# Where w_out's small sums are issued, and how many splits stand behind each half product of the output projection

## The chip, the core and the metric

The kernel runs on one core of a Trainium2 chip. The metric is device microseconds (us) of one execution. TensorE (PE in the profile) multiplies matrices, VectorE (DVE), ScalarE (ACT) and GpSimd (POOL) work elementwise. SyncE (SP) issues loads and stores; POOL also issues DMAs, those that add to what stands at the target (accumulating DMAs). Each engine takes its instructions in the order in which they are written.

## The reference

One layer of a gated short-convolution mixer between two RMS norms, in float32, for 1024 rows of 1024 channels:

```
u = rms_norm(x, pre_norm)
z, bg, cg, v = split(u @ w_in, 4)            # 1024 -> 4 x 2048
y = bg * causal_dwconv(cg * v, conv_w) * silu(z)
out = x + rms_norm(y @ w_out, post_norm)     # 2048 -> 1024
```

## The kernel before

Every float32 operand of a matmul is split into a high part (cast by ACT) and a low part (what the cast left over, by DVE); a product takes three matmuls, low by high, high by low, high by high. Both projections are made with fewer products than the plain way needs (a Strassen-like scheme): sums of blocks of the operands are multiplied instead of the blocks.

**Input projection.** The 64 column groups of `w_in` (16 channel blocks `c`, four kinds each) are taken three at a time: 20 *triples* `t` after four plain groups at the start. A triple is 20 steps `s`, each one product of six 128x512 matmuls into one of five PSUM chains pV, pW, pX, pY, pZ; ACT or DVE reads a chain before the next product is added to it. The weights of triple `t+1` are prepared during triple `t`: POOL makes 16 groups of sums (`sums`, L166 to L197, one source line each, L181 for group 0 to L196 for group 15), and ACT and DVE split the results in pairs named A to J (`split_w`, L219; A, B and C still in triple `t`, D to J in triple `t+1`). POOL also multiplies the gates (L314, L323, L341). `y` of each finished channel block goes to DRAM (`y_half`, stores by SP), and POOL adds up there the sums of `y` blocks that the output projection needs (`more`, L371).

**Output projection.** Its seven pairs of operands are called a, b, c, e, d, f, g. All but f are two half products `(i, h)` of four row tiles with 12 matmuls of 128x512 each, 48 in a half product. f is a further such scheme of seven parts p on quarter blocks, in the order `FP` = 1, 2, 6, 5, 7, 3, 4, 24 matmuls of 128x256 each; their results stand in three banks pf, read by DVE after each part (L1011, L1013). Parts of f need small sums of `w_out` blocks (`tf_d` in DRAM, made by `small_t`, L427) and of `y` blocks (`sf_d`, `small_s`).

`small_t` has four steps. Step 0: SP copies four quarter blocks of `w_out` to `tf_d`, 512 KB each. Step 1: POOL adds another quarter block to two of them. Step 2: POOL adds one of the results to a third block; it waits for step 1 to land. Step 3: POOL adds that to the fourth; it waits for step 2. Before, they stand in triple 18 (`END - 1`), at steps 2, 15, 18 and 20.

An operand of the output projection is a list of *pieces*, two of u (w_out side) and two of y for a half product, one of each for a part of f, 62 in all. `fetch_unit` loads raw pieces by SP, `ru_` for w_out and `ry_` for y; `split_unit` takes the next piece in order and issues its cast on ACT (L905, or L902 with a sign) and its low part on DVE (L906 or L903). `refill` loads ahead, never more than four pieces further than what is split. The first eight splits (a) stand in triple 19. After that, a fixed number of splits stands in the program behind each half product: four, or two behind each part of f. What is read out of PSUM (`combine`) comes behind these splits; behind f's parts 3 and 4 come the norms and the output rows of the first four row tiles (`finish_row`, DVE lines L96 to L104, L1050, L1070). Raw pieces share six buffers, split pieces and `ry_` tiles share 18.

Of the kernel before, what the change touches and what calls it, by code (L numbers as in the profile page):

```python
# [20 lines left out]
def kernel(  # L21
# [144 lines left out]
    def fetch_triple(t):  # L166
        if t < len(TRIPLES):
            for j, g in sorted(zip(COLS[t], TRIPLES[t]), key=lambda a: (2, 0, 1).index(a[0])):
                ws[t, j] = fetch_w(*g)
# [46 lines left out]
    def run_lows():  # L216
        while lows:
            lows.pop(0)()

    def split_w(t, unit):  # L220

        if t >= len(TRIPLES):
            return
        at = {"w0": ws[t, 0], "w1": ws[t, 1], "w2": ws[t, 2], "e": es[t]}
        x = wp.tile([P, 2, 2 * FC], F32R, tag="w", name=f"w{unit}_{t}", bufs=5)
        ps = bank(f"w{unit}_{t}")
        (i, a, m), (j, b, n) = UNITS[unit]
        if a == b and n == m + 1:
            src = flat(at[a][:, m : n + 1])
            nc.scalar.copy(ps, src)  # L230
            nc.scalar.copy(x[:, 0], src)  # L231
        else:
            nc.scalar.copy(ps[:, :FC], at[a][:, m])
            nc.scalar.copy(ps[:, FC:], at[b][:, n])
            nc.scalar.copy(x[:, 0], ps)  # L235
        lows.append(lambda: nc.vector.tensor_sub(x[:, 1], ps, x[:, 0].bitcast(F32)))  # L236
        wf[t, i], wf[t, j] = (x, 0), (x, FC)

    def product(t, i):

        ch, first = CHAIN[i]
        if first:
            banks[t, ch] = bank(f"p{ch}_{t}")
        x, off = wf.pop((t, i))
        for kk in range(2):
            s = slice(off + kk * P, off + (kk + 1) * P)
            pass3(banks[t, ch], x[:, 0, s], x[:, 1, s], U[i], kk, first and kk == 0, kk == 1)
# [27 lines left out]
    def run_due(at_once=False):  # L275
        moved = True
        while moved:
            moved = False
            for item in list(waiting):
                needs, gives, delay, do = item  # L280
                if all(n in have for n in needs):
                    if at_once or now[0] >= max(have[n] + delay.get(n[1], 0) for n in needs):
                        waiting.remove(item)
                        do()
                        have[gives] = now[0]
                        moved = True
# [59 lines left out]
    def read(t, i):  # L346

        ps = banks[t, CHAIN[i][0]]
        for (col, h), sign in READS.get(i, ()):
            c, ty = TRIPLES[t][COLS[t].index(col)]  # L350
            if (col, h) == (0, 1):
                use(c, ty, h, ps, sign, direct=True)
                continue
            if (t, col, h) not in acc:
                a = acc[t, col, h] = target(c, ty, h)
                if sign > 0:
                    nc.scalar.copy(a, ps)  # L357
                else:
                    nc.scalar.mul(a, ps, -1.0)  # L359
                continue  # L360
            a = acc[t, col, h]
            if sign > 0:
                nc.vector.tensor_add(a, ps, a)  # L363
            else:
                nc.vector.tensor_sub(a, a, ps)  # L365
            if LAST[col, h] == i:
                use(c, ty, h, acc.pop((t, col, h)))


    def more(dst, src):  # L370
        nc.gpsimd.dma_start(dst, src, accum_op=ALU.add)  # L371
# [6 lines left out]
    def run_later():  # L378
        if later and later[0][0] <= now[0]:
            later.pop(0)[1]()  # L380
# [23 lines left out]
    def fetch_t(j):  # L404
        for i, k, e in (("e", 0, 0), ("d", 0, 1), ("c", 1, 1), ("g", 1, 0)):
            nc.sync.dma_start(t_d[:, TK[i], j], wov[:, k * CH + j, e * HB : (e + 1) * HB])
# [14 lines left out]
    def w22(i, j):  # L421
        return quarter(wov, i, j, CH, HB)
# [4 lines left out]
    def small_t(step):  # L427
        if step == 0:
            for n, src in enumerate((w22(0, 0), w22(0, 0), w22(1, 1), w22(1, 0))):
                nc.sync.dma_start(tf_d[:, n], src)  # L430
        elif step == 1:
            more(tf_d[:, 0], w22(0, 1))
            more(tf_d[:, 2], w22(0, 1))
        elif step == 2:
            more(tf_d[:, 1], tf_d[:, 2])
        else:
            more(tf_d[:, 3], tf_d[:, 1])
# [173 lines left out]
    def high_u(i):  # L611
        U[i] = u = new_u(f"u_{i}")
        for kk in range(2):
            if i in FORM:
                nc.scalar.copy(u[:, 0, kk], FORM[i][kk])
            else:
                nc.scalar.copy(as_block(u[:, 0])[:, kk], stage(i)[:, kk])

    def low_u(i, eng=nc.vector, kks=(0, 1)):
        u = U[i]  # L620
        for kk in kks:
            if i in FORM:
                nc.vector.tensor_sub(u[:, 1, kk], FORM[i][kk], u[:, 0, kk].bitcast(F32))
            else:
                eng.tensor_sub(as_block(u[:, 1])[:, kk], stage(i)[:, kk], as_block(u[:, 0])[:, kk].bitcast(F32))
        FORM.pop(i, None)
# [208 lines left out]
    def first_chunk(s):  # L835

        if s == 4:
            silu1.append(snap(2, 1))
        elif s == 5:
            for h, t in ((0, sn0[2]), (1, silu1[0])):  # L840
                nc.gpsimd.tensor_mul(cv_of(0, h), cv_of(0, h), t)
        elif s == 6:
            gate_y(0, 0, sn0[3], 1, False)
        elif s == 19:
            gate_y(0, 1, plain_ps[3, 1], 1, True)

    FP = (1, 2, 6, 5, 7, 3, 4)
# [63 lines left out]
        OP[side, i, h, q] = t  # L911

    END = len(TRIPLES) - 1
    SUMS = {1: (0,), 2: (1,), 3: (2,), 4: (3,), 5: (4,), 6: (5,), 7: (6,), 8: (7,), 9: (8,), 10: (9,), 11: (10,), 12: (11,), 17: (12, 13), 18: (14,), 19: (15,)}
    SPLIT = {2: "D", 3: "E", 6: "F", 8: "G", 9: "H", 11: "I", 13: "J"}
    SPLIT_0 = {1: "F", 2: "G", 6: "H", 7: "E", 11: "I", 13: "J"}
# [5 lines left out]
    for t in range(len(TRIPLES)):  # L922
        for s, i in enumerate(ORDER if t else ORDER_0, 1):
            now[0] += 1
            product(t, i)
            read(t, i)
            run_lows()
            while low_us:
                low_us.pop(0)()
            if t == 0:  # L930
                first_chunk(s)
                if s in LOWS:
                    low_u(LOWS[s][0], kks=LOWS[s][1])
            run_due()
            for unit in (SPLIT if t else SPLIT_0).get(s, ""):
                split_w(t, unit)
            if t == 0 and s in HIGHS:
                high_u(HIGHS[s])
            for unit in (NEXT if t else NEXT_0).get(s, ""):
                split_w(t + 1, unit)  # L940
            sums(t + 1, (SUMS if t or s > 15 else SUMS_0).get(s, ()))
            if s == 14:
                fetch_triple(t + 2)
            if s in (7, 14, 20):
                run_later()
            if 2 <= t < 2 + 2 * CH:
                j = (t - 2) // 2
                if t % 2 == 0 and s == 3:
                    fetch_t(j)
                if t % 2 == 0 and s == 15:  # L950
                    add_t(j, 0)
                if t % 2 == 1 and s in (15, 20):
                    add_t(j, 1 + (s == 20))
            if t == END - 1 and s in (2, 15, 18, 20):
                small_t((2, 15, 18, 20).index(s))
            if t == END - 1 and s == 14 or t == END and s in (2, 8, 13, 15, 17):
                fetch_unit()
            if t == END and s in (6, 9, 11, 13, 15, 17, 19, 20):
                split_unit(True)
# [133 lines left out]
    def finish_row(t):  # L1093
        finish_o(t)
        if t + 2 < NT:
            load_res(t + 2)

    SMALL_S = {("c", 0): 0, ("c", 1): 1, ("e", 0): 2, ("e", 1): 3}
    for n, (i, h) in enumerate(OUT[:-2]):
        if (i, h) == ("f", FP[0]):  # L1100
            load_res(0)
            load_res(1)
        if i == "f":
            small_mm(h)
        else:
            for q in range(TH):
                out_mm(i, h, q)
        for z in range(2 if i == "f" else 4):
            split_unit()
            refill()  # L1110
        if (i, h) in SMALL_S:
            small_s(SMALL_S[i, h])
        if i != "f" and h == 1:
            for q in range(TH):
                combine(i, q)
        if i == "f" and h in (3, 4):
            for q in (0, 1) if h == 3 else (2, 3):
                norm_square(q, 1)
                finish_row(q)
# [33 lines left out]
```

## Time and profile before

| | us |
|---|---|
| median of 3 runs (lowest, highest) | 782.32 (779.84, 782.43) |
| the profiled execution | 782.2 |
| its span | 780.4 |
| PE busy in the span | 761.1 |
| triple 18, triple 19, first matmul | 552.3, 579.5 |
| first matmul of a, f, g | 615.5, 724.6, 744.7 |
| last matmul ends | 773.4 |

The profiled execution takes 1.8 us more than its span. Times in the text are us from the start of the span. In rows of the timeline the columns are start, duration, engine, line, operation, output<-inputs, count, and in brackets how long the engine sat idle before and what ended that. Views of waits give total, number, longest. In a table by windows each engine has its busy time and its instructions, then the granted TensorE clock, the share of the 16 DMA engines in use, and GB/s. q1 is SP's DMA queue, q0 POOL's.

### The profile page before, as it was taken

The page shows a single profiled execution, that of the slowest core. Times are in us where ns is not written, and L with a number is a line of the kernel's source. Part 1 is how long each engine was busy: PE and PEld are TensorE (multiplying, and loading weights), DVE is VectorE, ACT ScalarE, POOL GpSimd, SP SyncE. Part 2 cuts the span into 40 slices and gives each one's busy share as a digit, 9 for nine tenths or more (in the row PEclk, how much of TensorE's full clock was granted, in tenths as well). Part 3 has the DMA queues.
Part 4 walks back from the last instruction along what each step waited for, and adds up shares of the span by engine and source line. Part 5 has one row for each costly group of instructions (what it writes and reads, how often), then busy time and mean ns, then how long its engine had stood idle before and what let it go on. Part 6 is the DMA issues. An engine that isn't in the chain of part 4 may idle for free.

```text
span 780.4 us, 10226 instructions
## 1 busy us (share of the span) xinstructions
PE 761.1 (98%) x3458; PEld 632.6 (81%) x3458; DVE 498.4 (64%) x761; ACT 459.1 (59%) x887; POOL 471.3 (60%) x576
## 2 busy tenths in 40 slices
PE   9999999999999999999999999999999799999976
PEld 8888888888888888888888888888887588888965
DVE  6898766565656555664756575656654856456894
ACT  8869746555755665665565566657555554445641
POOL 0678978777876786696797869778853311100030
PEclk9999999999999999999999999999999899999998
DMA  9402346448165455364574763665768699967555
GB/s 326 134 1 68 95 126 145 135 85 231 37 188 122 133 140 132 95 161 122 122 203 81 178 146 95 149 175 112 206 116 213 220 343 393 299 175 257 207 197 203
DMA packets 111684, 128.10 MB, mean 164 GB/s; under 512 B 5080, under 2 KB 78096, under 8 KB 110864
## 3 DMA queue, kind: packets, MB, share of 16 engines
q1 hardware_dynamic: 99136, 104.37, 40.8%
q0 software_dynamic: 12480, 23.07, 18.0%
q8 instruction: 27, 0.44, 0.2%
q14 instruction: 25, 0.20, 0.1%
q10 hardware_dynamic: 16, 0.00, 0.0%
HBM read 108.56 MB, written 52.43 MB: 206 GB/s over the span
## 4 chain that ended last, share of the span: by engine, by line
PE 87%; DMA 4%; POOL 3%; DVE 2%; issue 2%; ACT 1%; SPq 0%; DVEq 0%; POOLq 0%; ACTq 0%
PE pX L135 7%; PE pX L136 7%; PE pX L137 7%; PE pY L136 6%; PE pY L135 6%; PE pY L137 6%; PE po_x L987 4%; PE po_x L988 4%; PE po_x L989 4%; PE pV L136 3%; PE pV L135 3%; PE pV L137 3%; PE pW L136 2%; PE pZ L136 2%; PE pW L137 2%; PE pZ L137 2%
## 5 line engine op out<-in xcount | busy, mean ns | idle before, releaser
L365 DVE TENSOR_TENSOR sn<-sn,pY 128x512 f32<-128x512 f32 x57 | 39.2, 687 | 56.4 <-PE pY L137 28.8
L341 POOL TENSOR_TENSOR g<-g,sn 128x512 f32<-128x512 f32 x29 | 40.6, 1406 | 35.0 <-ACT sn L339 28.1
L365 DVE TENSOR_TENSOR sn<-sn,pX 128x512 f32<-128x512 f32 x57 | 39.3, 689 | 33.6 <-PE pX L137 33.5
L314 POOL TENSOR_TENSOR g<-sn,g 128x512 f32<-128x512 f32 x23 | 30.0, 1305 | 44.1 <-DVE sn L363 44.1
L339 ACT ACTIVATE sn<-sn 128x512 f32<-128x512 f32 x24 | 15.2, 632 | 63.1 <-DVE sn L365 39.1
L359 ACT ACTIVATE sn<-pV 128x512 f32<-128x512 f32 x38 | 20.6, 596 | 48.0 <-PE pV L137 48.0
L1051 POOL TENSOR_TENSOR res<-xr,res 128x512 f32<-128x512 f32 x4 | 6.8, 1706 | 65.9 <-DVE res L1050 65.9
L323 POOL TENSOR_TENSOR g<-g,sn 128x512 f32<-128x512 f32 x20 | 28.3, 1414 | 19.2 <-DVE sn L365 18.9
L357 ACT COPY sn<-pZ 128x512 f32<-128x512 f32 x19 | 11.2, 589 | 46.7 <-PE pZ L137 46.7
L371 POOL DMA_DIRECT2D s_d<-s_d x24 | 20.0, 835 | 21.5 <-DMA s_d<-y_d 13.8
L181 POOL TENSOR_TENSOR raw<-raw 128x256 f32<-128x256 f32 x40 | 32.3, 920 | 0.0
L363 DVE TENSOR_TENSOR g<-pY,g 128x512 f32<-128x512 f32 x15 | 10.4, 692 | 30.7 <-PE pY L137 30.7
L186 POOL TENSOR_TENSOR raw<-e,raw 128x256 f32<-128x256 f32 x40 | 28.8, 741 | 1.6
L182 POOL TENSOR_TENSOR e<-raw,raw 128x512 f32<-128x512 f32 x20 | 26.2, 1311 | 1.6
L135 PE MATMUL pp<-b,wn 128*128 128x512 f32 x62 | 24.6, 397 | 0.0
L136 PE MATMUL pp<-b,wn 128*128 128x512 f32 x62 | 24.4, 393 | 0.0
L137 PE MATMUL pp<-b,wn 128*128 128x512 f32 x62 | 24.2, 390 | 0.0
L304 DVE SCALAR_TENSOR_TENSOR g<-g,cw,cv 128x512 f32<-128x512 f32 x30 | 22.5, 749 | 1.7
L236 DVE TENSOR_TENSOR wE<-wE,wE 128x512 fp32r<-128x512 f32 x20 | 13.7, 687 | 14.0 <-ACT wE L235 14.0
L304 DVE SCALAR_TENSOR_TENSOR cv<-g,cw,cv 128x512 f32<-128x512 f32 x30 | 22.4, 748 | 0.0
L135 PE MATMUL pX<-b,wJ 128*128 128x512 f32 x40 | 16.3, 408 | 6.1 <-DVE sn L365 6.1
L236 DVE TENSOR_TENSOR wC<-wC,wC 128x512 fp32r<-128x512 f32 x20 | 13.8, 688 | 11.9 <-ACT wC L231 11.9
(409 smaller groups left out, 2961.3 us busy)
## 6 DMA issues: line engine op xcount, KB each, us to landing
raw<-in_sc_w_in SPq DMA_DIRECT2D x64, 512.0 KB, 4.5
t_d<-in_sc_w_out SPq DMA_DIRECT2D x32, 256.0 KB, 4.4
s_d<-g SPq DMA_DIRECT2D x29, 256.0 KB, 2.1
s_d<-s_d POOLq DMA_DIRECT2D x24, 256.0 KB, 4.7
y_d<-g SPq DMA_DIRECT2D x23, 256.0 KB, 2.6
t_d<-in_sc_w_out POOLq DMA_DIRECT2D x16, 256.0 KB, 7.4
t_d<-t_d POOLq DMA_DIRECT2D x16, 256.0 KB, 5.0
xr<-in_x SPq DMA_DIRECT2D x8, 512.0 KB, 5.6
```

What stands on the lines that cost most here:

```text
L135: nc.tensor.matmul(ps, lo, u[:, 0, kk], start=first, stop=False, skip_group_check=True)
L136: nc.tensor.matmul(ps, hi, u[:, 1, kk], start=False, stop=False, skip_group_check=True)
L137: nc.tensor.matmul(ps, hi, u[:, 0, kk], start=False, stop=last, skip_group_check=True)
L181: 0: lambda: (add(w2[:, 0], w2[:, 0], w2[:, 1]), add(w2[:, 2], w2[:, 1], w2[:, 2])),
L186: 5: lambda: (sub(w0[:, 2], e[:, 3], w0[:, 2]), sub(w0[:, 0], e[:, 3], w0[:, 0])),
L304: nc.vector.scalar_tensor_tensor(g if j == TAPS - 1 else ps, g, tap(c, j), ps, op0=ALU.mult, op1=ALU.add)
L314: nc.gpsimd.tensor_mul(g, src, g)
L341: when([(c, "cv", h), (c, "silu", h)], (c, "z", h), {"cv": 1, "silu": 1}, lambda: nc.gpsimd.tensor_mul(cv_of(c, h), cv_of(c, h), t))
L365: nc.vector.tensor_sub(a, a, ps)
L987: nc.tensor.matmul(ps, lo, u[:, 0, k % 2], start=first, stop=False, skip_group_check=True)
L988: nc.tensor.matmul(ps, hi, u[:, 1, k % 2], start=False, stop=False, skip_group_check=True)
L989: nc.tensor.matmul(ps, hi, u[:, 0, k % 2], start=False, stop=last, skip_group_check=True)
```

## The change

```diff
@@
     END = len(TRIPLES) - 1
+    SMALL_T = ((END - 2, 3), (END - 1, 2), (END - 1, 6), (END - 1, 10))
...
-            if t == END - 1 and s in (2, 15, 18, 20):
-                small_t((2, 15, 18, 20).index(s))
+            if (t, s) in SMALL_T:
+                small_t(SMALL_T.index((t, s)))
@@
+    SPLITS = {("e", 0): 5, ("e", 1): 5, ("d", 0): 6, ("d", 1): 6, ("f", 3): 0, ("f", 4): 0}
+    SPLITS.update({("f", p): 2 for p in FP[:4]})
+    SPLITS["f", 7] = 0
...
-        for z in range(2 if i == "f" else 4):
+        for z in range(SPLITS.get((i, h), 4)):
             split_unit()
             refill()
```

The four steps of `small_t` move from triple 18's steps 2, 15, 18, 20 to triple 17's step 3 and triple 18's steps 2, 6, 10. On SP the four copies now stand in front of the three `w_in` loads of triple 19 instead of behind them and three stores. Behind e's half products stand five splits each instead of four, behind d's six, behind f's first four parts two each as before, and none behind its last three. So f's part 1 is split behind e, its parts 2, 6, 5 and 7, 3, 4 behind d, and g's eight pieces behind f's parts 1, 2, 6 and 5, in front of the output rows. SP's two loads of x rows now come behind the loads of g's first half.

POOL, from the end of triple 18's sums to triple 19's first gate, before (`raw_`, `e_`: weights and sums of triple 19; `g_0_5063`, `g_1_5038`: gates of channel block 14):

```order
L192 TENSOR_TENSOR raw_0_5168<-e_5257,raw_0_5168 128x256
L371 DMA s_d<-s_d 128x512
L371 DMA tf_d<-in_sc_w_out 128x4x256 x2
L341 TENSOR_TENSOR g_1_5038<-g_1_5038,sn_0_1_5375 128x512
L193 TENSOR_TENSOR e_5257<-e_5257,raw_3_5172 128x256
L194 TENSOR_TENSOR raw_3_5172<-raw_3_5172 128x256
L341 TENSOR_TENSOR g_0_5063<-g_0_5063,sn_0_0_5253 128x512
L195 TENSOR_TENSOR e_5257<-e_5257,raw_1_5170 128x256
L371 DMA tf_d<-tf_d 128x1024
L196 TENSOR_TENSOR raw_1_5170<-raw_1_5170 128x256
L371 DMA s_d<-s_d 128x512
L371 DMA tf_d<-tf_d 128x1024
```

Behind the last of these stands the gate `L323 g_0_5063`. POOL now, from the second group of sums on:

```order
L182 TENSOR_TENSOR e_5261<-raw_0_5172,raw_1_5174 128x512
L371 DMA tf_d<-in_sc_w_out 128x4x256 x2
L183 TENSOR_TENSOR e_5261<-e_5261,raw_1_5174 128x256
L184 TENSOR_TENSOR raw_3_5176<-raw_0_5172,raw_3_5176 128x256
L266 MEMSET g_0_5316 128x2
L185 TENSOR_TENSOR e_5261<-raw_3_5176 128x256
L186 TENSOR_TENSOR raw_1_5174<-e_5261,raw_1_5174 128x256 x2
L371 DMA tf_d<-tf_d 128x1024
L187 TENSOR_TENSOR raw_1_5174<-raw_1_5174 128x256
```

and further on:

```order
L190 TENSOR_TENSOR raw_0_5172<-raw_3_5176,raw_0_5172 128x256
L371 DMA tf_d<-tf_d 128x1024
L191 TENSOR_TENSOR raw_3_5176<-raw_3_5176,e_5261 128x256
L192 TENSOR_TENSOR raw_0_5172<-e_5261,raw_0_5172 128x256
L371 DMA s_d<-s_d 128x512
L341 TENSOR_TENSOR g_1_5038<-g_1_5038,sn_0_1_5378 128x512
```

The four `tf_d` DMAs that stood behind the sums of groups 0 to 11 now stand among them, the last in front of groups 10 and 11.

DVE around f's last parts, before (`pf_`: read of a part of f; `ou_g`, `oy_g`: low parts of g's pieces), first the piece with g's first six splits, and then the one with its last two; between the two pieces stand the output rows of tiles 0 and 1:

```order
L906 TENSOR_TENSOR ou_g_6631<-ru_g_6568,ou_g_6631 128x1024
L906 TENSOR_TENSOR ou_g_6634<-ru_g_6570,ou_g_6634 128x1024
L1011 TENSOR_TENSOR res<-pf_6500,res 128x2x256
L906 TENSOR_TENSOR oy_g_6666<-ry_g_6603,oy_g_6666 128x1024
L906 TENSOR_TENSOR oy_g_6669<-ry_g_6603,oy_g_6669 128x1024
L1013 TENSOR_TENSOR res<-res,pf_6605 128x2x256
L903 SCALAR_TENSOR_TENSOR ou_g_6699<-ru_g_6637,ou_g_6699 128x1024
L903 SCALAR_TENSOR_TENSOR ou_g_6702<-ru_g_6639,ou_g_6702 128x1024
```

```order
L1070 SCALAR_TENSOR_TENSOR res<-res,rs_post_6731,xr 128x512
L1013 TENSOR_TENSOR res<-res,pf_6500 128x2x256
L906 TENSOR_TENSOR oy_g_6768<-ry_g_6672,oy_g_6768 128x1024
L906 TENSOR_TENSOR oy_g_6771<-ry_g_6672,oy_g_6771 128x1024
L96 TENSOR_SCALAR ve_post_6777<-so,so_all 128x1
```

DVE at the same place now (its line numbers are one higher):

```order
L1014 TENSOR_TENSOR res<-res,pf_6564 128x2x256
L906 TENSOR_TENSOR oy_g_6590<-ry_g_6508,oy_g_6590 128x1024
L906 TENSOR_TENSOR oy_g_6593<-ry_g_6508,oy_g_6593 128x1024
L1014 TENSOR_TENSOR res<-res,pf_6528 128x2x256
L903 SCALAR_TENSOR_TENSOR ou_g_6623<-ru_g_6560,ou_g_6623 128x1024
L903 SCALAR_TENSOR_TENSOR ou_g_6626<-ru_g_6562,ou_g_6626 128x1024
L1012 TENSOR_TENSOR res<-pf_6629,res 128x2x256
L906 TENSOR_TENSOR oy_g_6655<-ry_g_6596,oy_g_6655 128x1024
L906 TENSOR_TENSOR oy_g_6658<-ry_g_6596,oy_g_6658 128x1024
L1012 TENSOR_TENSOR res<-pf_6528,res 128x2x256
L1014 TENSOR_TENSOR res<-res,pf_6629 128x2x256
L96 TENSOR_SCALAR ve_post_6714<-so,so_all 128x1
```

All low parts of g's pieces now stand in front of the first output row (L96), two between the reads of f's parts 1, 2, 6, 5 and 7.

## The prediction

> **What bounds the kernel now.** I read the page first, then PE's waits, then busy time by stretches, and then the chain of waits over the two places where PE stood still.
>
> ```profile
> PE 761.1 (98%) x3458; PEld 632.6 (81%) x3458; DVE 498.4 (64%) x761; ACT 459.1 (59%) x887; POOL 471.3 (60%) x576
> ```
> ```profile
> PE pX L135 <- DVE sn L365: 6.1, 1, 6.1
> PE po_x L987 <- DVE oy_g L906: 4.9, 1, 4.9
> ```
> ```profile
> 610.20:616.20 6.00, 5.99 (x14) 4.70 (x15) 4.95 (x5) 4.18 (x6) 2.77 (x3) 0.51 0.70 261
> 752.50:756.20 3.70, 3.69 (x9) 2.95 (x10) 3.56 (x12) 0.33 (x2) 1.04 (x1) 0.54 0.67 238
> ```
>
> PE is the bound: it has no wait of size but two, 6.1 and 4.9 us. Behind each it ran on a granted clock of 0.51 for 6.0 us and 0.54 for 3.7 us, which loses 6.0 x 0.49 = 2.9 and 3.7 x 0.46 = 1.7 us. So 6.1 + 2.9 + 4.9 + 1.7 = 15.6 us is all that this change can win: 8.9 in triple 19 and 6.6 in g, rounded. The number of matmuls doesn't change. The Trainium skill ("TensorE: Matmul & The Clock Gate", section "Part 1: The HAM clock gate (the "warmup" mystery)") has the half clock follow an idle window of about 3.4 us; both rows agree, and no run here shows a shorter wait of PE next to that limit.
>
> The chain through the first wait, and through the second:
>
> ```profile
> 593.92 9.46 DMA ry_a<-y_d
> 603.40 1.06 ACT oy_a L905
> 609.56 0.61 DVE sn L365
> 610.21 0.79 PE pX L135
> ```
> ```profile
> 731.06 7.75 DMA ry_g<-y_d
> ...
> 752.51 0.77 PE po_x L987
> ```
>
> First wait: the load of a's y pieces is issued at 593.92 and lands at 603.4. ACT stands at its cast, DVE behind ACT, and the read of pX that PE needs for the last two products is queued on DVE behind the low part of that piece: 610.21 - 603.38 = 6.8 us from landing to PE. Second wait: g's first twelve matmuls ran, and the low part of the second half's y piece came late, since on DVE the output rows of tiles 0 and 1 stand in front of it.
>
> **Triple 18 and 19.** Why is the load late? POOL, before:
>
> ```profile
> 558.67 0.73 POOL L183 TENSOR_TENSOR e<-e,raw 128x256 f32<-128x256 f32 x1
> 566.22 0.74 POOL L191 TENSOR_TENSOR raw<-raw,e 128x256 f32<-128x256 f32 x1
> 568.39 1.55 POOL L371 DMA_DIRECT2D tf_d<-in_sc_w_out  x1
> 576.54 1.25 POOL L371 DMA_DIRECT2D tf_d<-in_sc_w_out  x1 [6.61 <-issue]
> 583.78 0.88 POOL L371 DMA_DIRECT2D tf_d<-tf_d  x1 [1.20 <-DMA tf_d<-in_sc_w_out]
> 590.84 0.81 POOL L371 DMA_DIRECT2D tf_d<-tf_d  x1 [4.66 <-DMA tf_d<-tf_d]
> 591.38 1.60 POOL L323 TENSOR_TENSOR g<-g,sn 128x512 f32<-128x512 f32 x1
> ```
>
> The gate L323 stands behind the fourth DMA, which waited 4.66 us for the third. SP stores the gate's result and then issues ry_a, 593.92 - 591.38 = 2.5 us after the gate starts. Between the four starts lie 8.15, 7.24 and 7.06 us: the second waits 6.61 us for nothing that the profile names, and its start is 8.15 us behind the first, so I take it that POOL holds it until the first is through; the others wait for a landing. In program order these waits are unavoidable wherever the four stand. What changes is what is queued behind them.
>
> The change puts the first at the place of L183, 558.67, 9.7 us earlier; its data are there, since SP has nothing to wait for in front of the four copies. With the same distances the fourth starts at 581.1 instead of 590.84. But behind it now stand the sums of groups 10 and 11, a DMA, two gate products (L341), the groups 12 to 15 and a DMA. L191 (group 10) starts 0.54 us behind the fourth, the time from the fourth to L323 above: at 581.7, and it ends at 582.4, where it ended at 567.0. Who waits for that?
>
> ```profile
> 577.58 0.62 ACT L231 CAST wC<-raw 128x512 fp32r<-128x512 f32 x1
> 581.04 1.09 ACT L359 ACTIVATE sn<-pV 128x512 f32<-128x512 f32 x2 [2.84 <-PE pV L137]
> ```
> ```profile
> 583.56 0.39 PE L135 MATMUL pV<-u,wC 128*128 128x512 f32 x1
> 584.92 0.39 PE L135 MATMUL pY<-b,wC 128*128 128x512 f32 x1
> ```
> ```profile
> 579.76 0.69 DVE L321 SCALAR_TENSOR_TENSOR g<-pX,g 128x512 f32<-128x512 f32 x1 [0.83 <-PE pX L137]
> ```
>
> ACT's two instructions for wC (about 1.1 us) start at 582.4 and its read of pV (1.1) is queued behind them, so it ends at 584.6. PE needs that read for the product at 583.56: 1.0 us late. On POOL L192 and a DMA follow (1.2 us), then the gate L341 of 1.6 us like L323, to 585.2; the DVE gate L321, which needs it, ends at 585.9 and the read of pY behind it at 586.5, against 584.92 + 1.0 for the product that needs it: another 0.6. Cost 1.6 us. It grows one for one if the fourth DMA is later, and is nothing if it is 1.6 us earlier (range 0 to 4). The weights for A and B are late too but needed later than they come.
>
> From the fourth DMA to the gate L323 are now its 0.54 us, six sums (L191 to L196) of 0.74, two gate products of 1.6 and two DMAs of 0.54, 9.3 us in all: the gate starts at 590.4, only 1.0 us earlier than before, and ry_a is issued at 592.9. So the early issue is hardly the gain. The landing is:
>
> ```profile
> s_d<-g SPq DMA_DIRECT2D x1, 256.0 KB, 5.9
> ```
> ```profile
> q0 software_dynamic: 92, 0.30, 57.1%
> ```
> ```profile
> s_d<-g SPq DMA_DIRECT2D x29, 256.0 KB, 2.1
> ```
>
> The store just in front of ry_a took 5.9 us where the 29 of its kind take 2.1, and in the window 590 to 594 only POOL's queue moved anything (0.30 MB, the only queue listed): the fourth DMA, 512 KB, in flight until 598. It now lands near 588, and beside ry_a only one accumulate of 256 KB is left. I take 6 to 8 us for ry_a, 7.0, between 9.46 less the 3.8 us by which the store is over its median, and the 9.46 itself. It lands at 599.9, PE can go on at 606.7. Unhindered PE would be there after 18 products of 1.36 us (583.56 to 584.92) from triple 19's start at 579.5, at 604.0, plus 1.6: 605.6. A wait of 1.1 us is left (0 with a landing in 5.9 us, 3.6 with one in 9.46, and then the slow stretch comes back). Triple 19 wins 8.9 - 1.6 - 1.1 = 6.2 us.
>
> The Trainium skill ("DMA: Bandwidth & Descriptors", section "Anatomy of one DMA — SWDGE (gpsimd) path") gives a POOL-issued DMA about 2.0 us plus its bytes at 436 GB/s, for 512 KB an estimate of 3.2 us. The trace's 7 to 8 us disagree, and the measurement decides; by the page the fourth would start near 568.3, both rests would be nothing, and the time, with the last stage as below, would be 767.7.
>
> On SP the four moved copies now stand ahead of triple 19's three weight loads. I cost them at nothing: four issues, each well under 1 us, in a triple of 27 us whose weights are wanted in the next one.
>
> **The last stage.** DVE during f, before:
>
> ```profile
> 727.66 0.69 DVE L1011 TENSOR_TENSOR res<-pf,res 128x512 f32<-128x512 f32 x1 [0.58 <-PE pf L1006]
> 728.27 1.22 DVE L906 TENSOR_TENSOR ou_f<-ru_f,ou_f 128x1024 fp32r<-128x1024 f32 x1
> 730.54 0.69 DVE L1013 TENSOR_TENSOR res<-res,pf 128x512 f32<-128x512 f32 x1
> ```
>
> ```profile
> 724.59 0.28 PE L1004 MATMUL pf<-ou_f,oy_f 128*128 128x256 f32 x1
> 744.74 0.40 PE L987 MATMUL po_x<-ou_g,oy_g 128*128 128x512 f32 x1
> ```
>
> One read and two low parts take DVE 730.54 - 727.66 = 2.88 us, just what PE takes for a part of f: (744.74 - 724.59) / 7 = 2.88. Before, 14 low parts stood here, six of f and eight of g, and the last two behind two output rows. Now the six stand behind d, and g's eight follow parts 1, 2, 6 and 5. If DVE starts as before, g's last low part ends at 727.66 + 4 x 2.88 = 739.2, and PE wants it at 752.5 - 4.9 = 747.6: the wait and its slow stretch are gone, 6.6 us.
>
> But DVE has no slack in this row of steps: part 6 needs the read of part 1 (one bank), 7 that of 6, 3 that of 5, 4 that of 7. What delays DVE's first read delays PE. And DVE reaches it only behind the six splits and d's four reads. The last of the six waits for the load of part 4's y:
>
> ```profile
> 710.28 1.22 DVE L906 TENSOR_TENSOR oy_f<-ry_f,oy_f 128x1024 fp32r<-128x1024 f32 x1
> ...
> 713.80 1.23 DVE L906 TENSOR_TENSOR oy_f<-ry_f,oy_f 128x1024 fp32r<-128x1024 f32 x1 [1.16 <-ACT oy_f L905]
> ```
> ```profile
> 715.05 0.38 SPq L870 DMA_DIRECT2D ry_f<-s_d  x1
> ```
> ```profile
> ry_f<-s_d SPq DMA_DIRECT2D x1, 512.0 KB, 8.5
> ```
> ```profile
> 716.63 0.69 DVE L1088 TENSOR_TENSOR res<-po_x,res 128x512 f32<-128x512 f32 x1 [1.61 <-PE po_x L989]
> 719.35 0.69 DVE L1088 TENSOR_TENSOR res<-po_x,res 128x512 f32<-128x512 f32 x1 [0.48 <-PE po_x L989]
> ```
>
> The load is issued when the split of 713.80 ends and frees its buffer. Now it needs the buffer freed two splits earlier, by the one of 710.28: 711.5. With 7 us (ry_g's 7.75 is near) to 8.5 us to land and two splits of 1.1 us the first read of d starts at 720.7 to 722.2 instead of 716.63. Each of d's four rounds takes 2.7 us, of which 0.48 is waiting, so 2.25 without: DVE is through at 729.7 to 731.2, and has read part 1 at 730.4 to 731.9. PE starts part 6 at 724.6 + 5.8 = 730.4, so it waits 0 to 1.5 us. I take 1.0 us (range 0 to 4). ry_g waits for a tile that d's last matmuls free, just ahead of 724.6, and lands by 724.6 + 7.75 = 732.3; its low parts stand behind part 2's read, which comes about then. That costs nothing. The last stage wins 6.6 - 1.0 = 5.6 us.
>
> **Sum.** 782.2 - 6.2 - 5.6 = 770.4 us against the profiled execution, which stands 0.1 us from the median of 782.32. For the waits of 1.0 to 1.5 us I add no slow stretch.
>
> **Rivals.** (1) Only the last stage wins. The waits among the sums and a landing of ry_a as slow as before cost what the early start gives: 782.2 - 5.6 = 776.6. For it speaks that the gate comes just 1.0 us earlier; against it the 5.9 us store, which shows what held the load. (2) Only triple 19 wins: DVE's row of steps in f starts 4 us late (the load of 8.5 us becomes one of 12) and passes that to PE with the slow stretch. 782.2 - 6.2 = 776.0. (3) Slower. POOL's chain among the sums takes as long as the same two shapes take later:
>
> ```profile
> 660.09 1.30 POOL L371 DMA_DIRECT2D sf_d<-s_d  x1 [5.97 <-issue]
> 670.23 1.27 POOL L371 DMA_DIRECT2D sf_d<-s_d  x1 [8.84 <-issue]
> 686.16 0.83 POOL L371 DMA_DIRECT2D sf_d<-sf_d  x1 [13.79 <-DMA sf_d<-sf_d]
> ```
>
> There 10.1 us lie between the first two and 15.9 to the third. With 10.1 and then twice 12 (half way between 7.1 and 15.9, rounded) the fourth starts at 592.8 instead of 581.1: PE waits 1.6 + 11.7 = 13.3 us for wC and what hangs on it, with a slow stretch of 2.9, and the rest of 1.1 stays: 17.3 lost where 8.9 was, and 5.6 won, 785.0. It decides from a fourth DMA 8 to 9 us late, about 590. Against it: those three ran beside the loads of the output projection's pieces. (4) Both repairs fail by halves (a PE wait of 4 us at each place, with the slow stretches of 2.9 and 1.7, and the 1.6 at wC: 14.2 of the 15.6 stay), 780.8: no difference that can be told.
>
> **How the numbers follow.** Forecast 0.54, rival 1 0.17, rival 2 0.11, rival 4 0.10, rival 3 0.08. A measurement of this kernel tells about 0.5% from no change, 3.9 us: faster is below 778.4. Faster 0.82, same 0.10, slower 0.08. The forecast's own range is 766 (all 15.6 won) to 775 (rests of 3 us at one place). The range given goes to 765.5, since the runs shown reach 2.4 us below the profiled one, and to 777.5, which takes in rivals 1 and 2.
>
> **What would show it.** The wait of PE for oy_g is gone and the clock is 1.0 behind g's first half. POOL's second tf_d DMA starts 8 us behind the first with 6 to 7 us of idle time, now between L182 and L183; L191 starts near 581.7. PE has a short wait at pV<-u,wC. ry_a is issued near 592.9 and lands by 600. DVE's first read of pf is 2 to 4 us later relative to the start of f. I am wrong if POOL doesn't stand between the first two, if PE's wait in triple 19 stays above 4 us, or if waits over 3 us appear in f.

## The result, and the profile after

The changed kernel takes 769.33 us (median of 4 runs, 767.91 to 770.13) against 781.33 (4 runs, 779.84 to 782.43) for the kernel before: a ratio of 0.9846, 95% interval 0.982 to 0.9871. The forecast was 770.4 (765.5 to 777.5), with 0.82 for faster. Of all executions reported here one, of the kernel before beside e1 to e3, fell far out of line (2294.45 us): the medians take it in, the ratios leave it out.

The page of the changed kernel, then its waits of PE (total, times, longest):

```profile
span 767.9 us, 10230 instructions
...
PE 757.8 (99%) x3458; PEld 630.2 (82%) x3458; DVE 497.5 (65%) x761; ACT 459.1 (60%) x887; POOL 471.3 (61%) x576
```
```profile
PE pw L489 <- DVE idle L459: 1.1, 1, 1.1
PE pX L135 <- DVE sn L365: 0.2, 1, 0.2
```

Both waits of the kernel before are gone but for 0.2 us; the 1.1 us at L489 belong to the start of the kernel and were there before. The slow stretches behind them are gone too. These are the windows of the same lengths behind the two places (length, PE, PEld, DVE, ACT, POOL with their instructions, then the granted clock, DMA share, GB/s):

```profile
605.10:611.10 6.00, 5.99 (x26) 4.99 (x27) 4.95 (x5) 4.18 (x6) 2.78 (x3) 1.00 1.05 345
741.00:744.70 3.70, 3.70 (x18) 3.04 (x18) 2.72 (x8) 1.46 (x5) 1.74 (x1) 1.00 0.81 278
```

In 6.0 us PE does 26 matmuls where it did 14, and in 3.7 us 18 where it did 9, at a clock of 1.00.

Where the 12.5 us between the two spans (780.4 and 767.9) come from is read off the starts of PE's first matmuls of each stage:

| us | before | after | difference |
|---|---|---|---|
| up to triple 19 | 579.48 | 579.91 | +0.43 |
| triple 19 | 36.01 | 28.05 | -7.96 |
| a to d | 109.10 | 108.80 | -0.30 |
| f | 20.15 | 20.42 | +0.27 |
| g, first to last matmul's start | 28.31 | 21.56 | -6.75 |
| from there to the end | 7.35 | 9.16 | +1.81 |

The last row is what no term of the forecast held. POOL's `tf_d` DMAs in triple 18 and the two rows that the forecast named behind them, changed kernel (the rows between are left out):

```profile
558.97 1.26 POOL L371 DMA_DIRECT2D tf_d<-in_sc_w_out  x1
566.29 1.26 POOL L371 DMA_DIRECT2D tf_d<-in_sc_w_out  x1 [6.06 <-issue]
574.05 0.86 POOL L371 DMA_DIRECT2D tf_d<-tf_d  x1 [2.72 <-DMA tf_d<-in_sc_w_out]
579.76 0.81 POOL L371 DMA_DIRECT2D tf_d<-tf_d  x1 [1.03 <-DMA tf_d<-tf_d]
580.33 1.01 POOL L191 TENSOR_TENSOR raw<-raw,e 128x256 f32<-128x256 f32 x1
589.10 1.59 POOL L323 TENSOR_TENSOR g<-g,sn 128x512 f32<-128x512 f32 x1
```

The second DMA is held for 6 us again, now in the middle of the sums, and the distances are 7.32, 7.76 and 5.71 us (8.15, 7.24, 7.06 before). L191 starts at 580.3 (forecast 581.7), the gate L323 at 589.1 (forecast 590.4). The chain of waits from there:

```profile
591.63 6.64 DMA ry_a<-y_d
598.30 1.06 ACT oy_a L905
...
602.64 1.21 DVE oy_a L906
...
604.46 0.61 DVE sn L365
```

The load is issued 2.3 us earlier and takes 6.64 us instead of 9.46. From its landing at 598.27 to PE's product at 605.11 pass 6.8 us, as before.

The end, in the chain that ended last:

```profile
748.65 1.75 POOL res L1052
...
750.84 5.46 DMA xr<-in_x
...
756.39 0.75 DVE gx L1069
757.14 0.67 DVE res L1071
...
758.25 4.69 DMA xr<-in_x
...
763.04 0.62 DVE res L1062
```

PE's last matmul starts at 758.74, in the middle of this chain. It isn't PE that the end waits for: tile 5's x row is loaded when tile 3's output row has freed the buffer (750.84), tile 7's when tile 5's has (758.25), and the last tile's output waits for that.

### The profile page after: what moved, and what is told of

Same layout as the page of the kernel before. It is cut to its first block, busy times and chain, and to the rows that moved or that the text cites. A ratio compares the mean times of both kernels' runs of the same rounds, so it can differ in the third digit from the quotient of the medians.

```text
span 767.9 us, 10230 instructions
## 1 busy us (share of the span) xinstructions
PE 757.8 (99%) x3458; PEld 630.2 (82%) x3458; DVE 497.5 (65%) x761; ACT 459.1 (60%) x887; POOL 471.3 (61%) x576
## 4 chain that ended last, share of the span: by engine, by line
PE 88%; DMA 4%; POOL 3%; DVE 2%; issue 1%; ACT 1%; SPq 0%; DVEq 0%; POOLq 0%; ACTq 0%
PE pX L135 7%; PE pX L136 7%; PE pX L137 7%; PE pY L135 6%; PE pY L136 6%; PE pY L137 6%; PE pV L136 3%; PE pV L137 3%; PE pV L135 3%; PE po_x L989 3%; PE po_x L988 3%; PE po_x L990 3%; PE pW L136 2%; PE pZ L136 2%; PE pW L137 2%; PE pZ L137 2%
## 5 line engine op out<-in xcount | busy, mean ns | idle before, releaser
L339 ACT ACTIVATE sn<-sn 128x512 f32<-128x512 f32 x24 | 15.2, 632 | 58.3 <-DVE sn L365 34.3
L323 POOL TENSOR_TENSOR g<-g,sn 128x512 f32<-128x512 f32 x20 | 28.2, 1412 | 19.2 <-DVE sn L365 18.9
L231 ACT CAST wC<-raw 128x512 fp32r<-128x512 f32 x20 | 12.3, 617 | 14.9 <-PE pZ L137 14.9
```

The source lines that it names most:

```text
L323: nc.gpsimd.tensor_mul(cv, cv, src)
```

## The experiments

Times are medians. e1 to e3, a0 to e6, and e7 and e8 each shared a chip, where the kernel before had medians of 781.22, 782.04 and 780.86 us. "Triple 19" is from its first matmul to a's, "tail" from the start of the last matmul to the end, both from the profiled execution.

| run | us (lowest to highest) | triple 19 | tail |
|---|---|---|---|
| e1 sums only | 775.99 (773.36 to 776.51) | 30.07 | 7.37 |
| e2 splits only | 774.64 (773.33 to 777.7) | 33.02 | 8.38 |
| e3 late fourth | 773.75 (772.25 to 777.25) | 32.46 | 8.60 |
| a0 changed again | 768.86 (768.2 to 769.87) | 27.65 | 8.45 |
| e4 three x buffers | 768.26 (767.17 to 769.46) | 29.50 | 7.41 |
| e5 sums apart | 771.61 (768.38 to 773.25) | 31.28 | 8.98 |
| e6 both | 767.08 (766.82 to 770.17) | 27.28 | 7.40 |
| e7 sums early | 769.09 (767.59 to 769.17) | 27.26 | 8.56 |
| e8 sums early, three x | 766.98 (766.75 to 767.24) | 27.26 | 7.40 |

**e1 and e2: each half alone.**

```diff
-    SPLITS = {("e", 0): 5, ("e", 1): 5, ("d", 0): 6, ("d", 1): 6, ("f", 3): 0, ("f", 4): 0}
-    SPLITS.update({("f", p): 2 for p in FP[:4]})
-    SPLITS["f", 7] = 0
+    SPLITS = {("f", p): 2 for p in FP}
```
```diff
-    SMALL_T = ((END - 2, 3), (END - 1, 2), (END - 1, 6), (END - 1, 10))
+    SMALL_T = ((END - 1, 2), (END - 1, 15), (END - 1, 18), (END - 1, 20))
```

The first is e1, the second e2, both against the changed kernel.

> The small sums of w_out stand as in the changed kernel, the splits as before. Theory (two repairs that have nothing to do with each other): triple 19, from its first matmul to a's, takes 28.1 us as in the changed kernel (36.0 before), PE waits 4.9 us for oy_g in g with 3.7 us of half clock behind it, and the last matmul is followed by 7.4 us as before, not 9.2: 782.2 - 7.9 = 774.3 us. By the prediction's own terms (6.2 in triple 19) 776.0. Rival (everything behind triple 19 was late for the same reason, so that an early y repairs g too): no wait in g, 770 or less.

> The splits stand as in the changed kernel, the small sums of w_out as before. Theory: triple 19 takes 36.0 us with the wait of 6.1 us at pX and its half clock, f takes 20.4 us (20.15 before), g 21.6 (28.3 before), and from the last matmul to the end pass 9.2 us instead of 7.4, since the rows' x loads now end last: 782.2 + 0.3 - 6.7 + 1.8 = 777.6 us. Rival (the longer tail has to do with the small sums or with that one execution): tail of 7.4 us, 775.8.

e1 is 5.2 us below the kernel before on its chip (ratio 0.9918, 0.9887 to 0.9949) and e2 6.6 (0.9927, 0.9901 to 0.9953); together 11.8, where the whole change gives 12.0. That the medians add up so well is in part luck, since e2's profiled execution won 3.0 us in triple 19 too (see below). What shows two separate repairs is each stage by itself: e1 repairs triple 19 and leaves g as it was, e2 repairs g (21.56 us, no wait) and leaves the landing of ry_a at 9.46 us. e1's triple 19 took 30.1 us, not the 28.1 of the changed kernel, so its time is that of the prediction's own terms (776.0) and not the expected 774.3. It keeps the wait in g (5.2 us), and its tail is the old 7.4:

```profile
PE po_x L988 <- DVE oy_g L906: 5.2, 1, 5.2
PE pV L135 <- ACT sn L359: 1.5, 1, 1.5
...
PE pY L135 <- DVE sn L365: 0.3, 1, 0.3
```

The other two waits are those that the prediction put at wC, at 1.0 and 0.6 us: here the third DMA followed the second after 9.3 us instead of 7.8, the fourth came at 581.57, and the read of pV was late by 1.5. In the changed kernel's profiled execution the fourth came at 579.76, and only a gap of 0.15 us was left there, in front of the product into pY.

e2 has the tail of the changed kernel without the moved sums (8.4 us), so the longer tail comes with the splits. Its triple 19 took 33.0 us instead of the 36.0 expected. One low part on DVE took 4.32 us in it instead of 1.22, and PE's wait came in two pieces:

```profile
590.55 4.32 DVE L906 TENSOR_TENSOR ou_a<-ru_a,ou_a 128x1024 fp32r<-128x1024 f32 x1
```
```profile
PE pY L135 <- DVE sn L365: 2.1, 1, 2.1
PE pX L135 <- DVE sn L365: 1.4, 1, 1.4
```

ry_a landed in the same 9.46 us. As I read it, the early wait and the slow stretch behind it passed while that load was under way, so the later wait shrank to 1.4 us, and no slow stretch followed that. e2's runs lie in two groups, 773.3 to 774.6 and 776.9 to 777.7 (expected: 777.6); whether the upper one is the one without the stretched instruction, and what stretched it, stays open, since no run tried it.

**e3: the early issue without the clear queue.** The change is one number, `(END - 1, 10)` to `(END - 1, 20)`.

> As the changed kernel, but the fourth DMA of the small sums stands behind group 15 again, just in front of the gate L323, where before had it. Its source has long landed, so POOL does not wait for it and ry_a is issued as early as in the changed kernel or earlier (590.5 to 591.6); but the 512 KB are in flight just ahead of ry_a. Theory (the fourth DMA in flight is what holds the landing up): ry_a takes about 9.5 us again instead of 6.6, the s_d store in front of it over 4 us instead of 2, PE waits 2 to 3 us at pX: 771.5 to 772.5 us. Rival (only the early issue counts; the landing depends on what SP's own queue holds): ry_a takes 6 to 7 us, no wait at pX, 769 to 769.7.

The theory held, but the wait was larger than expected, and the time of 773.75 us lies above the expected 771.5 to 772.5. ry_a is issued at 591.58, 0.05 us before the changed kernel's, and lands 3.3 us later; from e3, the load in the chain, PE's wait, and the s_d store in front of ry_a (size, then us from issue to landing):

```profile
591.58 9.96 DMA ry_a<-y_d
```
```profile
PE pX L135 <- DVE sn L365: 3.4, 1, 3.4
```
```profile
s_d<-g SPq DMA_DIRECT2D x1, 256.0 KB, 6.4
```

In the changed kernel that store took 3.0 us. The window 590 to 594 of the prediction says little about it, since SP had nothing to move there until the store was issued at 593.01. The 3.0 us behind the store's issue say more (packets, MB, share). In e3 only POOL's queue moved anything in them, in the changed kernel SP's did too:

```profile
q0 software_dynamic: 157, 0.48, 120.8%
```
```profile
q1 hardware_dynamic: 224, 0.42, 52.5%
q0 software_dynamic: 119, 0.21, 42.4%
```

In before, too, only POOL's queue moved anything in the 3.0 us behind the store's issue (0.32 MB).

e3 also splits triple 19's gain: 36.0 to 32.5 us by the earlier issue, 32.5 to 27.7 or 28.1 by the free queue and what is saved of the slow stretch.

**e4: the tail.** Beside it a0, the changed kernel again.

```diff
-    xr = p2.tile([P, 2, D], F32, tag="xr", name="xr")
+    xr = p2.tile([P, 3, D], F32, tag="xr", name="xr")
...
-        if t + 2 < NT:
-            load_res(t + 2)
+        if t + 3 < NT:
+            load_res(t + 3)
...
+        if (i, h) == ("f", FP[3]):
+            load_res(2)
```

(and `t % 2` becomes `t % 3` in both places.)

> The changed kernel itself, beside the next three on the same chip: 769.3 us, 7.9 won in triple 19, 6.7 in g, 1.8 lost behind the last matmul.

> As the changed kernel, but the x rows of the output have three buffers instead of two, so that tile t+3's load is issued where tile t+2's was. Theory (the tail of 9.2 us is the chain: rows of tile 5 wait for x, free its buffer, tile 7's x is loaded): no wait of DVE for x behind 755, tail 7.4 us, 1.8 us faster than the changed kernel beside it, 767.5. Rival (the tail is long because 250 GB/s of loads and stores crowd the last 15 us, or because DVE has the rows of tiles 2 and 3 so late): the loads and stores are the same ones, so the tail stays within 0.5 us of 9.2.

The tail is 7.41 us against 8.45 beside it and 9.16 in the first profile; the same loads and stores are done, so the rival falls. For the last tile DVE now waits for ACT's sum of squares, as it did before the change, and not for its x:

```profile
761.44 0.70 DVE L1056 SCALAR_TENSOR_TENSOR po_x<-po_x,gpost 128x512 f32<-128x512 f32 x1 [1.48 <-ACT jk L1021]
...
762.80 0.62 DVE L1062 SCALAR_TENSOR_TENSOR res<-last,rs_post,xr 128x384 f32<-128x384 f32 x1
```

Two short waits for x, of 0.64 and 0.42 us, are left behind 755 at earlier tiles, where none was expected. The median moved by 0.6 us only, not 1.8: the tail of the changed kernel was not 9.2 in every execution, and the profiled execution of e4, its slowest, lost 1.6 us at wC (waits 1.3 and 0.3, the fourth DMA at 581.75). By the medians alone e4 can't be told from a0.

**e5 and e6: the four DMAs apart.** e6 is e5 with e4's three buffers.

```diff
-    SMALL_T = ((END - 2, 3), (END - 1, 2), (END - 1, 6), (END - 1, 10))
+    SMALL_T = ((END - 2, 3), (END - 1, 2), (END - 1, 6), (END - 1, 15), (END - 1, 18))
...
             more(tf_d[:, 0], w22(0, 1))
+        elif step == 2:
             more(tf_d[:, 2], w22(0, 1))
-        elif step == 2:
+        elif step == 3:
             more(tf_d[:, 1], tf_d[:, 2])
```

> As the changed kernel, but the four accumulating DMAs of the small sums stand apart: the first behind group 1, the second behind group 5, the third behind group 11, the fourth behind group 14. Theory (POOL holds the second until the first is through, which is not a cost of the DMA itself): the second starts at about 566.3 as in the changed kernel, but with under 1.5 us of idle time instead of 6.1; the third at 574, the fourth with hardly a wait, L191 ends about 10 us earlier than at 581.3, no wait of PE at wC or pX, triple 19 in 27.1 to 27.5 us instead of 28.1: 0.6 to 0.9 us faster than the changed kernel beside it. Rival (each second DMA of this shape costs POOL its 6 us wherever it stands): again 6 us of idle time in front of the second, and the same in front of the DMA of y sums behind it; no gain, or a loss of up to 1 us.

> The changed kernel with both: three x buffers and the four DMAs apart. Theory: the gains add, 1.8 + 0.7 = 2.5 us faster than the changed kernel beside it, 766.8 us. Rival: with the tail as bound, only the larger counts, 767.5.

On POOL the theory held: the second DMA starts at the same time, but POOL comes to it 3.6 us later and idles that much less, if not under the expected 1.5 us (e5):

```profile
559.00 1.28 POOL L371 DMA_DIRECT2D tf_d<-in_sc_w_out  x1
566.59 1.26 POOL L371 DMA_DIRECT2D tf_d<-in_sc_w_out  x1 [2.52 <-issue]
...
571.78 0.74 POOL L191 TENSOR_TENSOR raw<-raw,e 128x256 f32<-128x256 f32 x1
```

POOL is thus held until the first is through, 7.2 to 7.9 us from start to start in the executions of e1 and e3 to e6 and of the changed kernel; no fixed price is paid at the second. The landings agree: in all eleven profiles the first took 6.9 to 8.1 us to land, and the second started 0.3 to 0.4 us behind that. A DMA of 256 KB isn't held in this way: in e8 one starts at 540.07, 1.5 us behind the first of the four. On the time the forecast for e5 failed: the third came at 578.24 instead of 574, the fourth waited 2.1 us for it, came at 586.23 and was in flight until 593.4 beside ry_a, and that took 8.81 us:

```profile
PE pX L135 <- DVE sn L365: 2.1, 1, 2.1
```

In e6, the same order, it came at 584.55, ry_a was issued 1.8 us earlier and took 7.6, and PE didn't wait. So this placement stands just at the edge, and e5's runs spread over 4.9 us. e6's 767.08 us lie between the 766.8 of its theory and the 767.5 of its rival, and as e5 by itself won nothing, it can't be told from them whether the gains add.

**e7 and e8: all four out of the way.** In place of e5's table, and e8 with three buffers:

```diff
+    SMALL_T = ((END - 2, 3), (END - 2, 6), (END - 2, 12), (END - 1, 2), (END - 1, 8))
```

> As the changed kernel, but the four accumulating DMAs of the small sums stand apart and two of them a triple earlier: behind groups 5 and 11 of triple 18's sums (in triple 17), behind group 1 and group 7 of triple 19's. Theory (triple 19 loses only what POOL's waits among the sums do to wC, and what a transfer of POOL's queue beside ry_a does to its landing): the fourth is issued before 570 and through before 580, no wait of PE in triple 19 over 0.3 us, triple 19 in 27.2 to 27.4 us in every run, s_d's store in front of ry_a in under 3.5 us, ry_a in under 6.6; the tail stays at 8.4 to 9.2. 0.5 to 1 us faster than the changed kernel's 768.9 to 769.3, about 768.2, and less spread from run to run. Rival (ry_a's 6.6 us and the rest of the waits come from SP's own loads, and the DMAs now beside triple 19's weight loads make those late): a wait of PE in triple 18 or at the start of triple 19, no gain.

> The same with three x buffers. Theory: triple 19 in 27.2 to 27.4 us and a tail of 7.4 us: 8.7 + 6.6 of the 15.6 us are won, 766.8 us, 2.2 faster than the changed kernel, every run within 1.2 us of the others. Rival (as above): 768 or more.

Both have no wait of PE in triple 19, 27.26 us for it, and e8 the 7.4 us tail: 766.98 us, five runs within 0.5 us of each other, 13.9 below the kernel before on its chip (0.982, 0.9796 to 0.9843). The changed kernel was measured on other chips only: it is 2.35 us slower in the first measurement and 1.9 in a0, where the kernel before was slower too, by 0.5 and 1.2. Beside the kernel before on the same chip e8 thus gains 1.9 and 0.7 us more than the changed kernel. Two details were missed: e7's median is hardly better than the changed kernel's (769.09; its tail was 8.6 and f took 20.5 us), and the s_d store took 4.2 us in e7 and 4.0 in e8, not under 3.5. The gate that ry_a stands behind starts 7 us earlier (e8):

```profile
560.48 0.81 POOL L371 DMA_DIRECT2D tf_d<-tf_d  x1
566.98 1.06 POOL L371 DMA_DIRECT2D tf_d<-tf_d  x1
569.57 0.74 POOL L191 TENSOR_TENSOR raw<-raw,e 128x256 f32<-128x256 f32 x1
582.25 1.59 POOL L323 TENSOR_TENSOR g<-g,sn 128x512 f32<-128x512 f32 x1
```

## Why the prediction was right, point by point

**What can be won.** "15.6 us is all that this change can win" held: 8.9 in triple 19 and 6.6 in g. The best version, e8, takes 27.26 us for triple 19 and 21.56 for g, which is 8.75 and 6.75 us less than before. It gains 15.2 us of span.

**Triple 19 (forecast 6.2, measured 7.96 in the first profile, 8.36 in a0).** The mechanism was right: POOL held at the second DMA, waits among the sums, wC late, ry_a issued a little earlier and landing much faster. Two sizes were off. The chain of the four took 20.8 us where 22.45 was assumed from the rows of before, so wC cost 0.15 us instead of 1.6, and the rest at pX was 0.2 to 0.4 instead of 1.1. e1 and e4, where the fourth came at 581.6 to 581.75, show what the forecast (581.1, cost 1.6) had drawn: waits of 1.3 to 1.5 and 0.3. So the working described an execution that does occur; the profiled one was faster. That "the early issue is hardly the gain" was half wrong: the issue came 2.3 us earlier, not 1.0, and e3 shows that this is worth some 3.5 of the 8 us with its part of the slow stretch; the landing, 4.4 to 4.8, is the rest. The four copies on SP, put at nothing, took 5.4 us to issue instead of 2.7, and PE has no wait behind them.

**The price of a POOL-issued DMA.** The Trainium skill ("DMA: Bandwidth & Descriptors", section "Anatomy of one DMA — SWDGE (gpsimd) path") gives about 2.0 us plus the bytes at 436 GB/s, and the prediction's estimate by it had the fourth at 568.3. It stood at 579.8, and the four took 5.3 to 9.9 us each to land in the eleven profiles, so the traces disagree, and the measurement decides.

**The last stage (forecast 5.6, measured 6.75 - 0.27 - 1.81 = 4.67).** Wait and slow stretch in g went as forecast. DVE's first read of pf came 2.1 us later relative to the start of f (5.13 instead of 3.07), as forecast, but cost PE only 0.1 to 0.4 us instead of 1.0. The step that failed is one that isn't in the text: what would be late next, once the wait is gone, was asked of f and not of the rows behind g. In before the first output row was made 26.3 us ahead of the last matmul's start (746.71 and 773.05), in the changed kernel 19.7 (739.02 and 758.74). The 6.6 us between them are PE's wait and its slow stretch, and in before they gave the x rows' two buffers time to turn over. With them gone the loads of x are the end: 1.0 to 1.8 us. e2 shows that it comes with the splits, e4 that it goes with a third buffer.

**The sum.** 770.4 against 769.7 for the profiled execution: the errors of +1.8 in triple 19 and -0.9 in the last stage partly cancel, so that the closeness of the sum is in part luck.

**The rivals.** (1), only the last stage, and (2), only triple 19, both fall: e1 and e2 give a share each. (3), the slow chain, falls: distances up to 9.3 us do occur (e1, e4), but in this order the fourth came at 581.8 at the latest, far from 590. (4) falls: no wait over 3 us is left.

## What to carry to other kernels

When the bound engine's wait is removed, look at every resource that had been using the wait to catch up, to the very last instruction: here two x buffers that kept pace only because PE stood still. A transfer that isn't on the path can be on it by its queue: move it in time, not only ahead in the order, and spread dependent DMAs so that the issuing engine never reaches one before the last is through. An order with a small margin can show as a spread from run to run (e5: 4.9 us, e8: 0.5; a fourth DMA 1.7 us later is what e5's profile has against e6's), and a forecast from one execution draws one point of it.

## What the runs showed of the hardware

**The clock gate.** Waits of 1.3 to 1.5 us in e1, e2 and e4 left the granted clock at 1.00, while waits of 2.1 us already cost a slow stretch of 3.1 to 3.3 us (e5, e2). The windows behind the wait of 1.3 us (e4) and of 2.1 us (e5):

```profile
585.52:589.00 3.48, 3.21 (x13) 2.34 (x14) 2.29 (x4) 2.92 (x7) 3.40 (x5) 1.00 0.93 148
```
```profile
606.80:609.93 3.13, 3.13 (x7) 2.46 (x8) 2.99 (x3) 1.32 (x3) 0.71 (x1) 0.51 1.05 408
```

In e2 the drop came 0.8 us after its wait of 2.1 us had ended. The Trainium skill ("TensorE: Matmul & The Clock Gate", section "Part 1: The HAM clock gate (the "warmup" mystery)") puts the half clock behind an idle window of about 3.4 us. These runs disagree: 2.1 us were enough.

**POOL's queue ahead of SP's.** While 512 KB of POOL's accumulating DMA were under way, a 256 KB store of SP took 5.9 and 6.4 us (before, e3) instead of 3.0, and the y load of 1024 KB behind it 9.5 to 10.0 instead of 6.6, with POOL's queue alone moving data for at least 3.0 us behind the store's issue.
